# Two weight sums of a Strassen-Winograd pair traced together and pinned in VectorE's order

## The chip, the cores and the metric

One core of a Trainium2 chip runs one launch of the kernel. The metric is device time in microseconds. The kernel before took 2118.74 us (median of three runs, 2118.1 to 2118.84).

## What is computed

One encoder layer on 1024 tokens of width 2048, all in fp32:

```
mod = silu(c) @ w_ada + b_ada;  shift, scale, gate = split(mod, 3)
h = rmsnorm(x, pre_g) * (1 + scale) + shift
q, k, v, gate_a, u, gate_p = split(h @ w_in)          # 4608 columns
y_a = windowed_gqa(q, k, v, rel_table, sink) * silu(gate_a)   # 8 heads, window 128
y_p = multiscale_pool(u, w_pool_grp, pool_scale) * silu(gate_p)
g_a, g_p = split(sigmoid(h @ w_merge + b_merge))      # 2 x 2048 columns
merged = g_a * (y_a @ w_br_attn) + g_p * (y_p @ w_br_pool)
out = x + gate * rmsnorm(merged @ w_out, post_g)
```

## The kernel before

Every big product is done in fp32 precision by splitting each operand into two float32r parts, `hi` and `lo`, and adding three products (hi·hi, hi·lo, lo·hi). A split (`split`, lines 95 to 100) is one ScalarE copy that makes `hi` and one VectorE subtraction that makes `lo`. On top of that each block of 256 output columns, called a *pair*, is one step of Strassen-Winograd multiplication on 2 x 2 blocks: seven block products where plain multiplication has eight. The generator `strassen` (lines 213 to 298) makes a pair. The moving operands (the seven combinations of the activations, `B11`, `T3`, `T2`, `B21`, `T4`, `T1`, `B22`) are prepared once and stay; the weights are loaded for every pair as four blocks A11, A21, A12, A22 in two tiles called `raw`, and the sums of them that the products need are made on VectorE:

- the first product, B11, takes A11 itself;
- the second, T3, takes S3 = A11 - A21, made at line 265 into a tile called `ws`;
- the third, T2, takes A21 + A22 - A11, made by an addition into A21 (line 267) and a subtraction into A11 (line 268);
- the others take A12, A22, the sum in A21, and A12 less the sum in A11.

`prep` splits such a block, giving tiles `whi` and `wlo` (four buffers each, so weights are split some three products ahead of TensorE). `product` runs its matmuls: with four tiles of 128 rows (nj = 4) twelve matmuls of 512 columns, first eight with `whi`, then four with `wlo`. `first_weights` (lines 260 to 269) is a generator that yields the weights of the first three products in turn; the work for S3 is traced when T3's weights are asked for.

Pairs come in stages. Ten half-depth pairs (nj = 2) open the program; then 29 pairs with nj = 4 do the first half of the depth of the combined projection (pass 1), 34 do the second half and add the first (pass 2), and 16 do the two branch projections. 79 pairs thus have nj = 4. `run` (line 325) steps a pair through seven places. At place 2 it finishes the product B22 of the pair before, so that TensorE sees B11, T3, B22 of the pair before, T2, B21, T4, T1. At chosen places it also runs a step of side work: in pass 1 weighted column sums of the modulation weights (`weigh`, line 500), in pass 2 the attention, unit by unit (`step`, line 1087), and then the pooling. In the attention stretch side steps stand at places 0, 1, 3, 4 and 6. A step of attention transposes the probabilities of the unit before (PT, line 1060), forms its scores (SCORE, lines 1037 to 1039, two PSUM banks), takes their maximum on VectorE (line 1043), the exponential on ScalarE (line 1046), a sum with the sink's share (lines 1047, 1048), a reciprocal on VectorE (line 1049) and a scaling on ScalarE (line 1050); every other step also multiplies by the values (PV, lines 1070 to 1072).

The order of each engine's instructions is set by the scheduler of the tile layer, which may move an instruction ahead of others if nothing that it depends on forbids it. `keep` (line 91) forbids it for one instruction: it is placed behind the instruction that was traced just before it on its engine. The weighings of pass 1 are all kept so, and with them what is kept behind them.

Of the kernel before, what the change touches and what calls it, by code (L numbers as in the profile page):

```python
# [43 lines left out]
def encoder_layer(ctx: ExitStack, tc: tile.TileContext, x, c, table, w_ada, b_ada, pre_g,  # L44
# [32 lines left out]
    def uid(s):  # L77
        cnt[0] += 1
        return f"{s}_{cnt[0]}"

    def bank(tag, name="b"):
        return psum.tile([P, 512], F32, tag=tag, name=uid(name), bufs=1 if tag in SEEDED else 2)
# [8 lines left out]
    def keep(ins):  # L91

        tc.keep_in_program_order(ins)

    def split(hi, lo, src, pin=False):
        ins = (nc.scalar.activation(hi, src, AF.Copy),  # L96
               nc.vector.tensor_tensor(lo, src, f32(hi), ALU.subtract))  # L97
        if pin:
            keep(ins[0])
            keep(ins[1])  # L100

    def add(o, a, b, eng=None):
        return (eng or nc.vector).tensor_tensor(o, a, b, ALU.add)  # L103

    def sub(o, a, b):
        return nc.vector.tensor_tensor(o, a, b, ALU.subtract)
# [74 lines left out]
    def load_raws(w, n0, rows, js, pin=False):  # L181

        raws = []
        nj = len(js)
        joint = wp.tile([P, 2, nj, 256], F32, tag="raw", name=uid("raw"), bufs=4) if nj < 4 else None
        for kh in range(2):
            r = joint[:, kh] if nj < 4 else wp.tile([P, nj, 256], F32, tag="raw", name=uid("raw"), bufs=4)
            ins = load(r, rows(w, js, kh)[:, :, n0:n0 + 256])
            if pin:
                keep(ins)  # L190
            raws.append(r)
        return raws
# [13 lines left out]
    def load_parts(ev, part):  # L206
        parts = {}
        for blk in ("22", "21", "11", "12"):
            parts[blk] = ev.tile([P, 512], F32, tag="ev", name=uid("part"))
            load(parts[blk], part(blk))  # L210
        return parts

    def strassen(w, n0, rows, js, op, ev, finish, part=None, raws=None, given=()):

        nj = len(js)
        raws = raws or load_raws(w, n0, rows, js)
        a11, a21, a12, a22 = (raws[kh][:, :, nt * P:(nt + 1) * P] for kh in range(2) for nt in range(2))
        parts = load_parts(ev, part) if callable(part) else part

        def prep(src):
            hi = wp.tile([P, nj, P], F32R, tag="whi", name=uid("whi"), bufs=4)
            lo = wp.tile([P, nj, P], F32R, tag="wlo", name=uid("wlo"), bufs=4)  # L230
            split(hi, lo, src)
            return hi, lo

        def product(wts, mov, ps, fresh=False):
            hi, lo = wts
            for n, (w_, m_) in enumerate(((hi, 0), (hi, 1), (lo, 0))):
                for i, j in enumerate(js):
                    nc.tensor.matmul(ps, w_[:, i], op[mov][j][m_], start=fresh and i == 0 and n == 0,  # L238
                                     stop=i == nj - 1 and n == 2, skip_group_check=True)

        def new(name):
            return ev.tile([P, 512], F32, tag="ev", name=uid(name))

        def read(name, blk, ps):

            t = new(name)
            if part is None or name == "u2":
                nc.scalar.activation(t, ps, AF.Copy)  # L248
                ps = t
            if part is not None:  # L250
                add(t, ps, parts[blk])
            return t

        def result(blk, ps):
            if part is None:
                finish(blk, ps, None, new("c"))
            else:
                finish(blk, ps, parts[blk], parts[blk])

        def first_weights():  # L260
            yield from given
            if not given:
                yield prep(a11)
                s3 = wp.tile([P, nj, P], F32, tag="ws", name=uid("ws"))
                sub(s3, a11, a21)
                yield prep(s3)
            add(a21, a21, a22)
            sub(a11, a21, a11)
            yield prep(a11)

        wts = first_weights()
        pairs_[0] += 1
        bx, bz, bv = bank("mm", "X"), bank(SEEDED[pairs_[0] % 2], "Z"), bank("mm", "V")
        product(next(wts), "B11", bx, True)
        nc.scalar.activation(bz, bx, AF.Copy)
        yield
        product(next(wts), "T3", bv, True)
        p7 = read("p7", "22", bv)
        yield
        product(next(wts), "T2", bz)  # L280
        u2 = read("u2", "21", bz)
        yield
        product(prep(a12), "B21", bx)
        result("11", bx)
        sub(a12, a12, a11)
        yield
        product(prep(a22), "T4", bv)
        finish("21", bv, u2, u2)
        yield
        product(prep(a21), "T1", bz)  # L290
        u4 = new("u4")
        nc.scalar.activation(u4, bz, AF.Copy)
        add(p7, p7, u4)
        finish("22", None, None, p7)
        yield
        product(prep(a12), "B22", bz)
        result("12", bz)
        yield
# [177 lines left out]
    def modulation(j, tile_of, pin=False):  # L476

        st_ = {}

        def step(q, between=None):  # L480
            if q == 0:
                st_["pv"] = bank("at", "GEMV")
            pv = st_["pv"]
            for kc in range(4 * q, 4 * q + 4):
                g = kc % 4 * 32
                ins = nc.tensor.matmul(pv[g:g + 32, :], scz[:, kc, :], tile_of(kc), start=kc < 4,
                                       stop=kc >= 12, tile_position=(0, g))
                if pin:
                    tc.keep_in_program_order(ins)
            if q == 3:  # L490
                acc = xa2.tile([P, 4, P], F32, tag="acc", name=uid("acc"), bufs=2)
                tc.keep_in_program_order(
                    nc.scalar.activation(acc, pv.rearrange("p (g n) -> p g n", g=4), AF.Copy))
                if between:
                    between()
                mod_columns(j, sum_columns(acc))

        return [partial(step, q) for q in range(4)]
# [178 lines left out]
    s0, s1, s2, s3 = modulation(0, ada[0].__getitem__, True)  # L677
# [19 lines left out]
    s0, s1, s2, s3 = modulation(1, ada[1].__getitem__, True)  # L697
# [541 lines left out]
    for b, w in enumerate((w_ba, w_bp)):  # L1239
# [56 lines left out]
        for i in range(8):  # L1296
            def finish(blk, ps, addend, res, gates=gates, shut=shut, open_gate=open_gate, i=i, b=b):
                gt = gates.pop((i, blk))
                if ps is not None and addend is None:
                    keep(nc.vector.tensor_tensor(res, ps, gt, ALU.mult))  # L1300
                else:
                    if ps is not None:
                        add(res, ps, addend)
                    keep(nc.vector.tensor_tensor(res, res, gt, ALU.mult))
                if b == 0:
                    store(block(mp_d, i * 256)(blk), res)
                else:
                    dst = sums_to.pop((i, blk))
                    add(dst, dst, res)
                    if blk[1] == "2":  # L1310
                        store(block(m_d, i * 256)(blk), dst)
                    if to_sum:
                        fetch_sum(*to_sum.popleft())
                if shut:
                    open_gate()
                if wanted:
                    fetch_gate(*wanted.popleft())
# [321 lines left out]
```

## Time and profile before

| what | value |
|---|---|
| median of three runs | 2118.74 us |
| the profiled execution, its own time | 2117.89 us |
| its span, first to last instruction | 2116.1 us |
| TensorE busy, share of the span | 98% |
| VectorE busy | 73% |
| ScalarE busy | 52% |

Read it so: the span and the execution's own time differ by 1.8 us, which lie outside the instructions. In lines of the profile PE is TensorE's matmuls, PEld its weight loads, DVE VectorE, ACT ScalarE, POOL GpSimd, SP the queue of most DMAs. L106, L103, L97 and L96 are helper lines (subtraction, addition, the two halves of a split), so the names of the tiles tell which work it is. A grouped row ends in "busy us, mean ns of one | idle us before it and who ended it". Tile names are cut of their numbers there: `p<-p,u` is the addition of u4 to p7 after T1.

### The profile page before, as it was taken

How to read it: one execution, taken by the hardware profiler on the slowest of the kernel's cores; microseconds unless marked ns; L12 is line 12 of the kernel's file. 1: busy time of each engine (PE TensorE's matmuls, PEld its weight loads, DVE VectorE, ACT ScalarE, POOL GpSimd, SP SyncE). 2: the span in 40 equal slices, each digit the busy share in tenths (PEclk: the TensorE clock that was granted, in tenths of full speed). 3: DMA queues.
4: the chain of work that ended last, by engine and by line, in shares of the span. 5: the costliest groups of instructions: out<-in, count | busy, mean ns of one | idle time of the engine just before them, and what ended most of it. 6: DMA issues, size and time to landing. Idle time of an engine off the chain costs nothing.

```text
span 2116.1 us, 29011 instructions
## 1 busy us (share of the span) xinstructions
PE 2083.9 (98%) x9573; PEld 1715.0 (81%) x9573; DVE 1541.3 (73%) x2771; ACT 1106.8 (52%) x2106; POOL 20.1 (1%) x90
## 2 busy tenths in 40 slices
PE   6999999999999999999999999999999999999998
PEld 4688888888888888888888888888788788888887
DVE  5787667777546776677777677866957977879667
ACT  4654444443366544666655543333645644767554
POOL 0000000000000000000000000000000000000000
PEclk9999999999999999999999999999999999999999
DMA  9886666899767456544645476776755566686897
GB/s 330 278 268 226 205 192 208 292 306 324 255 194 238 149 177 203 171 158 158 197 149 163 156 230 216 219 233 197 237 173 160 184 193 194 220 316 217 294 321 249
DMA packets 302998, 468.20 MB, mean 221 GB/s; under 512 B 24138, under 2 KB 145122, under 8 KB 302848
## 3 DMA queue, kind: packets, MB, share of 16 engines
q1 hardware_dynamic: 299472, 457.82, 66.5%
q0 software_dynamic: 3040, 8.48, 1.0%
q8 instruction: 75, 1.23, 0.2%
q14 instruction: 75, 0.61, 0.1%
q10 hardware_dynamic: 336, 0.06, 0.0%
HBM read 341.45 MB, written 126.90 MB: 221 GB/s over the span
## 4 chain that ended last, share of the span: by engine, by line
PE 91%; DMA 5%; DVE 2%; ACT 1%; issue 1%; SPq 0%; DVEq 0%; POOL 0%; ACTq 0%; POOLq 0%
PE Z L238 31%; PE X L238 20%; PE V L238 20%; PE Z L1349 2%; PE Z L1351 2%; PE Z L1350 2%; DMA ada<-in_w_ada_dram 2%; DMA xt<-in_x_dram 1%; PE V L1351 1%; PE X L1351 1%; PE V L1349 1%; PE X L1349 1%; PE X L1350 1%; PE V L1350 1%; PE PT L1060 1%
## 5 line engine op out<-in xcount | busy, mean ns | idle before, releaser
L96 ACT ACTIVATE whi<-raw 128x512 fp32r<-128x512 f32 (+1 forms) x532 | 322.0, 606 | 508.8 <-PE Z L238 252.0
L97 DVE TENSOR_TENSOR wlo<-raw,whi 128x512 fp32r<-128x512 f32 (+1 forms) x532 | 347.8, 658 | 164.5 <-PE Z L238 122.7
L97 DVE TENSOR_TENSOR wlo<-wr,whi 128x512 fp32r<-128x512 f32 x224 | 150.6, 690 | 51.2 <-ACT whi L96 44.9
L96 ACT ACTIVATE whi<-wr 128x512 fp32r<-128x512 f32 x224 | 138.3, 629 | 86.0 <-DVE wlo L97 31.9
L103 DVE TENSOR_TENSOR raw<-raw,raw 128x512 f32<-128x512 f32 x79 | 54.6, 691 | 106.2 <-DMA raw<-in_w_merge_dram 82.0
L238 PE MATMUL V<-T3h,whi 128*128 128x512 f32 x334 | 91.4, 392 | 1.7 <-DVE u L103 1.2
L238 PE MATMUL Z<-T1h,whi 128*128 128x512 f32 x334 | 91.5, 392 | 0.9 <-ACT u L248 0.9
L238 PE MATMUL Z<-T2h,whi 128*128 128x512 f32 x334 | 91.2, 392 | 0.3 <-ACT whi L96 0.3
L238 PE MATMUL X<-B11h,whi 128*128 128x512 f32 x334 | 91.3, 391 | 0.0
L96 ACT ACTIVATE whi<-ws 128x512 fp32r<-128x512 f32 (+1 forms) x88 | 53.5, 608 | 72.0 <-PE X L238 63.9
L238 PE MATMUL Z<-B22h,whi 128*128 128x512 f32 x334 | 91.1, 392 | 0.0
L238 PE MATMUL V<-T4l,whi 128*128 128x512 f32 x334 | 90.7, 390 | 0.3 <-DVE T4l L97 0.2
L238 PE MATMUL X<-B21h,whi 128*128 128x512 f32 x334 | 90.8, 391 | 0.0
L238 PE MATMUL Z<-T2h,wlo 128*128 128x512 f32 x334 | 90.3, 390 | 0.5 <-DVE wlo L97 0.5
L238 PE MATMUL V<-T3l,whi 128*128 128x512 f32 x334 | 90.5, 390 | 0.2 <-DVE T3l L97 0.2
L238 PE MATMUL V<-T4h,whi 128*128 128x512 f32 x334 | 90.6, 391 | 0.0
L238 PE MATMUL Z<-T1l,whi 128*128 128x512 f32 x334 | 90.4, 390 | 0.1
L238 PE MATMUL X<-B11l,whi 128*128 128x512 f32 x334 | 90.4, 390 | 0.0
L238 PE MATMUL Z<-T1h,wlo 128*128 128x512 f32 x334 | 90.3, 390 | 0.0
L238 PE MATMUL X<-B11h,wlo 128*128 128x512 f32 x334 | 90.2, 390 | 0.0
L238 PE MATMUL Z<-B22l,whi 128*128 128x512 f32 x334 | 90.2, 390 | 0.0
L238 PE MATMUL X<-B21l,whi 128*128 128x512 f32 x334 | 90.2, 389 | 0.0
(358 smaller groups left out, 4840.4 us busy)
## 6 DMA issues: line engine op xcount, KB each, us to landing
part<-part_d SPq DMA_DIRECT2D x136, 256.0 KB, 5.1
ada<-in_w_ada_dram SPq DMA_DIRECT2D x128, 256.0 KB, 5.4
raw<-in_w_merge_dram SPq DMA_DIRECT2D x64, 512.0 KB, 5.8
raw<-in_w_in_dram SPq DMA_DIRECT2D x62, 512.0 KB, 4.2
wr<-ws_dS SPq DMA_DIRECT2D x60, 512.0 KB, 5.5
wr<-in_w_out_dram SPq DMA_DIRECT2D x48, 512.0 KB, 5.3
proj_d<-part SPq DMA_DIRECT2D x68, 256.0 KB, 2.2
sw<-in_w_out_dram SPq DMA_DIRECT2D x64, 256.0 KB, 6.1
```

The lines of the kernel that those rows point to most:

```text
L96: ins = (nc.scalar.activation(hi, src, AF.Copy), nc.vector.tensor_tensor(lo, src, f32(hi), ALU.subtract))
L97: nc.vector.tensor_tensor(lo, src, f32(hi), ALU.subtract))
L103: return (eng or nc.vector).tensor_tensor(o, a, b, ALU.add)
L238: nc.tensor.matmul(ps, w_[:, i], op[mov][j][m_], start=fresh and i == 0 and n == 0, stop=i == nj - 1 and n == 2, skip_group_check=True)
L1060: nc.tensor.transpose(pt[:, i * P:(i + 1) * P], p[:, i * P:(i + 1) * P], ident)
L1349: nc.tensor.matmul(pb, hi, w[0], start=first, stop=False, skip_group_check=True)
L1350: nc.tensor.matmul(pb, lo, w[0], start=False, stop=False, skip_group_check=True)
L1351: nc.tensor.matmul(pb, hi, w[1], start=False, stop=last, skip_group_check=True)
```

## The change

```diff
             if not given:
                 yield prep(a11)
                 s3 = wp.tile([P, nj, P], F32, tag="ws", name=uid("ws"))
-                sub(s3, a11, a21)
+                ins = sub(s3, a11, a21)
+                if nj == 4:
+                    keep(ins)
+                    keep(add(a21, a21, a22))
                 yield prep(s3)
-            add(a21, a21, a22)
+            if nj < 4:
+                add(a21, a21, a22)
             sub(a11, a21, a11)
             yield prep(a11)
```

In every pair with nj = 4 the subtraction that makes S3 is now kept behind the VectorE instruction traced just before it, and the addition into A21 is traced right behind that subtraction, and kept there, instead of being traced after S3's split. No instruction is added or taken away. Which instruction stands just before depends on `run`: where place 0 has no side step it is the `lo` half of A11's split; where it has one, it is the last VectorE instruction of that side step.

The listings below give each engine's instructions in their order, by source line; in those of after, lines behind the change have numbers higher by 4.

On VectorE, in pass 1, at a pair whose place 0 has a side step (its weights are raw_2068 and raw_2070, in the listing after raw_2069 and raw_2071; `p_509` is p7 of the pair before, `acc` the weighed sum). Before, the two sums stand far ahead, the subtraction first:

```order
L106 TENSOR_TENSOR ws_2185<-raw_2068 128x512
L103 TENSOR_TENSOR u_489_1935<-V_1869,u_489_1935 128x512
...
L103 TENSOR_TENSOR raw_2068<-raw_2068,raw_2070 128x4x128
...
L97 TENSOR_TENSOR wlo_2164<-raw_2068,whi_2163 128x512
L106 TENSOR_TENSOR raw_2068<-raw_2068 128x4x128
L97 TENSOR_TENSOR wlo_2188<-ws_2185,whi_2187 128x512
```

After:

```order
L97 TENSOR_TENSOR wlo_2164<-raw_2069,whi_2163 128x512
L103 TENSOR_TENSOR u_518_2090<-V_2006,u_518_2090 128x512
L509 SCALAR_TENSOR_TENSOR acc_1998<-ada_2001,sc,acc_1998 128x512 x2
L509 SCALAR_TENSOR_TENSOR acc_1998<-ada_2047,sc,acc_1998 128x512 x2
L103 TENSOR_TENSOR p_509_2043<-p_509_2043,u_528_2156 128x512
L106 TENSOR_TENSOR ws_2185<-raw_2069 128x512
L103 TENSOR_TENSOR raw_2069<-raw_2069,raw_2071 128x4x128
L97 TENSOR_TENSOR wlo_2189<-ws_2185,whi_2188 128x512
```

The subtraction has moved from ahead of the pair's A11 split to behind four weighings and behind the addition of u4, which needs the pair before to have finished T1.

On VectorE, in the attention stretch, at its second pair (weights raw_8514 and raw_8516; ISA rows are the maximum over scores and the read of its result). Before, the subtraction stands beside the attention step of a whole pair earlier:

```order
L103 TENSOR_TENSOR m_8156<-m_8156 128x1
L106 TENSOR_TENSOR ws_8568<-raw_8514 128x512
L1049 RECIPROCAL m_8156<-m_8156 128x1
...
L103 TENSOR_TENSOR raw_8514<-raw_8514,raw_8516 128x4x128
...
L97 TENSOR_TENSOR wlo_8530<-raw_8514,whi_8529 128x512
```

After, it stands behind the reciprocal of the step of its own place 0 (SCORE_8556, m_8561):

```order
L1047 ISA p_8560,m_8561<-SCORE_8556,bt_8006,nsink_t 128x384
L1047 ISA m_8561 128x1
L97 TENSOR_TENSOR pp_8491<-PT_8546,pp_8490 128x3x128
L1047 ISA p_8615,m_8616<-SCORE_8611,bt_8002,nsink_t 128x384
L1047 ISA m_8616 128x1
L103 TENSOR_TENSOR m_8561<-m_8561 128x1
L1053 RECIPROCAL m_8561<-m_8561 128x1
L106 TENSOR_TENSOR ws_8568<-raw_8514 128x512
L1086 TENSOR_TENSOR g_8225<-PV_8589,g_8225 128x128
L103 TENSOR_TENSOR raw_8514<-raw_8514,raw_8516 128x4x128
L1086 TENSOR_TENSOR g_8227<-PV_8589,g_8227 128x128
L97 TENSOR_TENSOR wlo_8572<-ws_8568,whi_8571 128x512
```

On TensorE, at the same pair, between the end of B11 and the first matmul of T3. Before, one transpose and one set of scores stand there:

```order
L238 MATMUL X_8526<-B11h_6822,wlo_8530 128x512
L1060 MATMUL PT_8546<-ident,p_8428 128x128 x3
L1037 MATMUL SCORE_8556<-k_8030,qhi_8552 128x384
L1038 MATMUL SCORE_8556<-k_8031,qhi_8552 128x384
L1039 MATMUL SCORE_8556<-k_8030,qlo_8553 128x384
L238 MATMUL V_8528<-T3h_6827,whi_8570 128x512
```

After, the attention work that stood behind T3, B22 and T2 has been drawn ahead of T3 by the scheduler: three more sets of scores, the nine PV matmuls and one more transpose:

```order
L1043 MATMUL SCORE_8556<-k_8031,qlo_8553 128x384
L1041 MATMUL SCORE_8611<-k_8031,qhi_8498 128x384
...
L1041 MATMUL SCORE_8667<-k_8031,qhi_8552 128x384
...
L1075 MATMUL PV_8589<-pp_8491,v_8142 128x256
L1076 MATMUL PV_8589<-pp_8490,v_8143 128x256
...
L1064 MATMUL PT_8605<-ident,p_8506 128x128 x3
L1041 MATMUL SCORE_8720<-k_8031,qhi_8498 128x384
...
L238 MATMUL V_8528<-T3h_6827,whi_8571 128x512
```

Over the whole program the subtraction stands, before, ahead of the u4 addition of the pair before it in all 79 pairs. After, it stands behind that addition in 21: six pairs of pass 1 (every other one of its first thirteen pairs), the first pair of pass 2, the 13 attention pairs, and the first pair of the first branch projection. In one of the 13 attention pairs (the sixth) the last VectorE instruction of place 0 is a gate multiplication that waits for little, and T3 follows its scores at once as before. In the first pair of the branch projection the subtraction stands behind the preparation of B21 and T4 of the new activations, and so behind the part addition that reads B22 of the pair before. In the other 58 pairs both sums stand right behind A11's split, one to three products ahead of T3.

## The prediction

> **What bounds the kernel now.** I read the page first: busy shares and the chain that ended last.
>
> ```profile
> PE 2083.9 (98%) x9573; PEld 1715.0 (81%) x9573; DVE 1541.3 (73%) x2771; ACT 1106.8 (52%) x2106; POOL 20.1 (1%) x90
> ...
> PE 91%; DMA 5%; DVE 2%; ACT 1%; issue 1%; SPq 0%; DVEq 0%; POOL 0%; ACTq 0%; POOLq 0%
> ```
>
> TensorE is busy for 98% and is 91% of the chain. VectorE, on which the change acts, is 2% of it. Then the table by stage, for the opening, for all pairs with nj = 4, and for the attention stretch (columns: length, then busy us of PE, PEld, DVE, ACT, POOL; then granted clock, DMA share, GB/s).
>
> ```profile
> 0.00:130.00 130.00, 109.06 (x558) 75.96 (x559) 89.73 (x216) 77.24 (x169) 3.61 (x46) 0.97 0.91 298
> 165.00:1800.00 1635.00, 1631.47 (x7506) 1355.82 (x7505) 1173.76 (x2091) 811.50 (x1522) 3.41 (x19) 1.00 0.64 205
> 880.00:1215.00 335.00, 334.13 (x1740) 286.67 (x1739) 245.73 (x624) 201.04 (x469) 0.14 (x2) 1.00 0.51 164
> ```
>
> From 165 to 1800 us TensorE is idle for 1635.00 - 1631.47 = 3.53 us in all. That bounds any gain: nothing the change does to VectorE can save more than 3.5 us, 0.17%. And TensorE has no slack there: each time a product waits for its weights the whole wait is added to the end. So the question is only whether T3, the product that S3 feeds, now waits.
>
> VectorE does wait for the weights' loads at these sums (who waited, for whom: us in total, times, longest):
>
> ```profile
> DVE raw L103 <- DMA raw<-in_w_merge_dram: 82.0, 27, 8.3
> ...
> DVE ws L106 <- DMA raw<-in_w_merge_dram: 25.4, 10, 5.0
> ```
>
> The sums stand so early in its order that loads have often not landed. Later sums will wait less, but these waits end long before TensorE needs anything, as the 3.53 us say; shortening them earns nothing.
>
> **The change, part by part.** No instruction is added, and no DMA is issued by the moved steps; two sums of some 0.69 us move within VectorE's order. In 58 of the 79 pairs they now stand right behind A11's split, a product or more ahead of T3. I cost these at nothing: a product takes 2.72 us (below), the two sums 1.3. The loads of later weights move by some places in SP's queue, since buffers come free a little differently; they were issued a pair ahead, and I cost that at nothing too, 0 to 1 us. If that cover were gone, the DMA waits above would pass to TensorE.
>
> *Attention, 12 pairs.* TensorE at the second attention pair, where T3 follows PT and SCORE at once:
>
> ```profile
> 919.39 0.49 PE L1060 MATMUL PT<-ident,p 128*128 128x128 f32 x3
> 919.64 0.42 PE L1037 MATMUL SCORE<-k,qhi 128*128 128x384 f32 x1
> ...
> 920.07 0.34 PE L1039 MATMUL SCORE<-k,qlo 128*128 128x384 f32 x1
> 920.25 1.08 PE L238 MATMUL V<-T3h,whi 128*128 128x512 f32 x4
> ...
> 922.98 0.28 PE L1070 MATMUL PV<-pp,v 128*128 128x256 f32 x1
> ...
> 924.06 0.49 PE L1060 MATMUL PT<-ident,p 128*128 128x128 f32 x3
> 924.31 0.42 PE L1037 MATMUL SCORE<-k,qhi 128*128 128x384 f32 x1
> ```
>
> The scores end at 920.07 + 0.34 = 920.41 and T3 starts at 920.25. After the change S3 cannot be made before these very scores have passed through maximum, exponential, sum and reciprocal. The same steps, one unit on, on VectorE and ScalarE:
>
> ```profile
> 921.46 0.61 DVE L1043 CUSTOM_DVE_ANT_0 p<-SCORE,bt,nsink_t 128x384 f32<-128x384 f32 x1
> ...
> 922.00 0.09 DVE L1043 DVE_READ_ACCUMULATOR2_ANT m<- 128x1 f32 x1
> ...
> 922.12 0.62 ACT L1046 ACTIVATE p<-p,m 128x384 f32<-128x384 f32 x1 [1.28 <-DVE m L1043]
> 922.64 0.19 ACT L1046 ACTIVATION_READ_ACCUMULATOR p<-p,m 128x1 f32 x1
> 922.73 0.28 ACT L1047 ACTIVATE m<-sink_t,m 128x1 f32<-128x1 f32 x1
> ...
> 923.04 0.16 DVE L103 TENSOR_TENSOR m<-m 128x1 f32<-128x1 f32 x1 [0.96 <-ACT m L1047]
> ...
> 923.24 0.17 DVE L1049 RECIPROCAL m<-m 128x1 f32<-128x1 f32 x1
> ```
>
> and the means of the rest over this stretch (pp is the probabilities' split, q the queries'):
>
> ```profile
> L97 DVE TENSOR_TENSOR pp<-PT,pp 128x384 fp32r<-128x384 f32 x48 | 26.5, 553 | 1.3 <-ACT pp L96 1.2
> L1050 ACT ACTIVATE p<-p,m 128x384 f32<-128x384 f32 x48 | 29.6, 617 | 7.5 <-DVE m L1049 7.5
> L1016 DVE SCALAR_TENSOR_TENSOR qlo<-qr,qhi 128x512 fp32r<-128x512 f32 x14 | 9.6, 688 | 0.0
> L106 DVE TENSOR_TENSOR ws<-raw 128x512 f32<-128x512 f32 x13 | 8.9, 687 | 0.0
> L1015 ACT ACTIVATE qhi<-qr 128x512 fp32r<-128x512 f32 x14 | 8.7, 624 | 0.0
> L96 ACT ACTIVATE whi<-ws 128x512 fp32r<-128x512 f32 x13 | 8.0, 618 | 0.1
> ```
>
> VectorE's new order there is maximum and read (921.46 to 922.09: 0.63), pp 0.55, the next maximum and read 0.63, addition and reciprocal (923.04 to 923.41: 0.37), S3 0.69: with a hop of 0.1 from TensorE, S3 is ready 2.97 us after the scores. ScalarE must by then have done the second exponential (begun when the second read ends, at 1.91; with its read 0.71) and the scaling (0.62): free at 3.25, then `whi` 0.62, and a hop of 0.1: T3 can start at 3.97 after the scores, 4.1 after its place before. (The hops are an estimate; 922.09 to 922.12 and 923.01 to 923.04 are 0.03.)
>
> TensorE fills part of this with the attention work drawn ahead: three score sets (919.64 to 920.25: 0.61 each), the PV set (922.98 to 924.06: 1.08), one PT (924.06 to 924.31: 0.25): 3.16 us. **T3 waits 4.1 - 3.16 = 0.95.** That order holds in 4 of the 12 pairs: 3.8 us. Three pairs have a third maximum and read ahead of the reciprocal (+0.63) and four score sets with two PTs as cover (2.44 + 1.08 + 0.50 = 4.02): 0.7, together 2.1. Three have a query split in the way, +0.69 on VectorE and up to two copies of 0.62 on ScalarE, behind the same 3.16 of cover or, with narrow scores at a sequence's end, less: 1.6, 1.6 and 2.4, together 5.6. One has a split of the values (+0.69) against some 3.4 of cover: 1.4. The last, which has no scores left to draw on, has the pp splits, S3 and `whi` (0.5 + 0.55 + 0.69 + 0.62 and hops) against one PT and a third of a PV set: 1.8. Sum for attention: **14.7 us**. From below it is 0, if the cover holds; from above 12 x 4.1 = 49, if none does. I take the sum, since each duration in it has a row.
>
> After T3 nothing is late: A11's second split follows within 3 us, and T2 is two products off.
>
> *Pass 1, six pairs.* The rows of one such place, and means of 300 to 480 us:
>
> ```profile
> 434.62 1.07 PE L238 MATMUL X<-B11h,whi 128*128 128x512 f32 x4
> ...
> 434.82 0.60 ACT L292 ACTIVATE u<-Z 128x512 f32<-128x512 f32 x1
> ...
> 437.34 1.07 PE L238 MATMUL V<-T3h,whi 128*128 128x512 f32 x4
> ```
>
> ```profile
> L505 DVE SCALAR_TENSOR_TENSOR acc<-ada,sc,acc 128x512 f32<-128x512 f32 x21 | 15.7, 748 | 0.1
> L103 DVE TENSOR_TENSOR p<-p,u 128x512 f32<-128x512 f32 x10 | 6.9, 689 | 0.0
> ```
>
> B11 starts when T1 ends and lasts 437.34 - 434.62 = 2.72. Behind it: u4's copy (0.20 + 0.60), the addition (0.69), S3 (0.69), `whi` (0.62), three hops: 3.1, so T3 waits 0.4. The four weighings ahead (4 x 0.75 = 3.0) start with T4's end, 2.72 before T1's, and can hold the addition by 0.1 to 0.2 more, a late load of theirs by more. I take 0.45 x 6 = **2.7** (0 to 9, a product's length of 1.5 at most each).
>
> *The first pair of the branch projection.*
>
> ```profile
> 1495.37 1.07 PE L238 MATMUL Z<-B22h,wlo 128*128 128x512 f32 x4
> ...
> 1498.09 1.07 PE L238 MATMUL V<-T3h,whi 128*128 128x512 f32 x4
> ```
>
> S3 now stands behind the addition that reads this B22. It ends at 1496.44; the addition, two subtractions and S3 take four times 0.69 less some overlap, to 1499.1, `whi` to 1499.8: 1.7 after T3's place. I take **1.7** (0 to 3). At the first pair of pass 2 the subtraction stands behind no such addition; 0.
>
> Sum: 14.7 + 2.7 + 1.7 = 19.1 us on the profiled execution's 2117.89, 2137.0; the median of the runs is 0.85 above that execution, so 2137.8, say **2137**.
>
> **The rivals.** *The cover holds (not slower).* If hops are nothing and a scaling goes ahead of the second exponential, or the drawn-ahead pieces run slower than in their old places, T3 finds S3 ready in attention. It decides at 4.1 us of work per pair between scores and T3: 3.16 to 4.02 stand there. For it: TensorE waits nowhere in this stretch now, behind the same chains. Then only pass 1 and the branch pair remain, 2118.74 + 4.4 at most, about 2121.
>
> *The cover fails.* The pieces drawn ahead need VectorE too: a third score set needs a bank that a maximum has emptied, PV needs the pp splits, PT the scaling. Where TensorE, which takes them in order, waits for each, nothing is covered: 49 + 4.4 gives 2172; half of it 2155. Against it: by the rows above the second maximum is done before the third score set is due.
>
> *The clock falls with the waits.* In the opening, with 21 us idle, the granted clock was 0.97 over 130 us, 3.9 us lost, 0.19 us for each idle us; 19 us of waits would cost 3.6 more: 2141. [...]
>
> *Faster, or the pin does nothing.* VectorE's 82 us of waits for loads shrink, but only 3.53 us of TensorE's idle time can come back: 2115.2 at best, within 0.2%.
>
> **How the numbers follow.** My measurement can tell 0.2% (4.2 us) from no change. Forecast, T3 waiting in attention, 2126 to 2150: 0.70. Cover holds, 2121: 0.12. Cover fails by half or more, 2155 to 2172: 0.11. Clock, 2141 or more: 0.04. Faster: 0.03. So slower 0.85, same 0.12, faster 0.03. The range, 2122 to 2157, leaves out part of the covered and half of the uncovered case.
>
> **What would show it.** TensorE's waits in 880 to 1240 us should grow from under 1 us to about 15, on the V matmuls that take T3 with `whi`, put down to ScalarE's split of `ws`, in 12 places of 0.5 to 2.5 us; pass 1 should show six waits of some 0.5 us. The stretches 1215 to 1450 and the last one should keep their lengths. The granted clock should stay 1.00. I am wrong if the waits fall on SCORE, PV or PT instead (cover fails), if VectorE's waits for loads turn up as TensorE's, or if T2 waits.

## The result and the profile after

The changed kernel takes **2139.14 us** (median of five runs, 2137.14 to 2139.89) where the kernel before takes 2118.74 (median of five, 2118.1 to 2121.35): 1.0092 times as long, 95% interval 1.0080 to 1.0104. The forecast was 2137. The profiled execution took 2139.84 us, with a span of 2138.0, 21.9 more than before.

The page of the changed kernel: busy shares, the engines of the chain that ended last, and two of the costliest groups.

```profile
PE 2095.1 (98%) x9573; PEld 1716.6 (80%) x9573; DVE 1545.3 (72%) x2771; ACT 1095.7 (51%) x2106; POOL 20.2 (1%) x90
...
PE 89%; DVE 3%; ACT 2%; DMA 1%; issue 1%; DVEq 0%; SPq 0%; ACTq 0%
...
L96 ACT ACTIVATE whi<-ws 128x512 fp32r<-128x512 f32 (+1 forms) x88 | 53.5, 608 | 100.4 <-DVE ws L106 63.2
L238 PE MATMUL V<-T3h,whi 128*128 128x512 f32 x334 | 93.7, 399 | 9.5 <-ACT whi L96 7.6
```

The last of these rows before the change:

```profile
L238 PE MATMUL V<-T3h,whi 128*128 128x512 f32 x334 | 91.4, 392 | 1.7 <-DVE u L103 1.2
```

The instructions are the same and the shares nearly so; TensorE is still 89% of the chain. What is new is in the last row: T3 waits 7.6 us for the split of `ws`, and that split in turn waits for `ws` itself (63.2 us, most of it harmless). The pairs with nj = 4 (length, busy us of PE, PEld, DVE, ACT, POOL, then granted clock, DMA share, GB/s):

```profile
165.00:1800.00 1635.00, 1620.66 (x7411) 1339.23 (x7410) 1161.51 (x2066) 789.00 (x1503) 3.42 (x19) 1.00 0.63 202
```

From 165 to 1800 us TensorE's idle time has gone from 3.53 to 14.34 us. That is 10.8 us; the span grew by 21.9. So half of the loss does not show as idle time. To find it I set the start of T1 in every pair against its start in the trace before; the difference is the lag up to that pair. This is worked out from the records of the two traces, with no line of a view that prints it:

| stretch | lag gained, us | forecast |
|---|---|---|
| opening, up to the first pairs (nothing changed there; -0.4 to 2.1 in the other kernels) | 0.62 | 0 |
| pass 1, all but its end | 6.46 | 2.7 |
| end of pass 1 (one pair's wait for ScalarE, -0.6 to 2.3 us in the other kernels) | 0.62 | 0 |
| attention | 13.16 | 14.7 |
| pairs behind attention | -0.87 | 0 |
| branch projections | 1.95 | 1.7 |
| sum | 21.94 | 19.1 |

In between the lag stays flat to 0.01 us for up to twelve pairs at a time: what the change costs falls in single pairs.

**Attention.** One window from T1 of the last pair without attention to T1 of the last one with it, before and after:

```profile
886.38:1219.27 332.89, 332.02 (x1727) 284.84 (x1725) 242.38 (x612) 196.43 (x457) 0.14 (x2) 1.00 0.51 165
```

```profile
894.08:1240.12 346.04, 340.68 (x1726) 284.93 (x1725) 241.06 (x615) 193.05 (x459) 0.14 (x2) 1.00 0.49 158
```

The window is 13.15 us longer: 4.49 us more idle (0.87 to 5.36) and 8.66 us more "busy" for as many matmuls (1727 and 1726) at the same clock of 1.00. A matmul's row ends some 0.16 us after the next one has started (PV below: starts 0.12 apart, 0.28 long), so a pause of up to that length leaves no idle time in the row. Counted from start to start in both windows, against the usual spacing of each kind of matmul, the pauses ahead of V matmuls grow by 5.5 us, ahead of PT by 2.8, of PV by 2.7 and of SCORE by 2.7; the rest changes by -0.6. Together these are the 13.15. The waits that do show, who waited for whom, in us, times, longest:

```profile
PE V L238 <- ACT whi L96: 2.2, 6, 0.7
PE PT L1064 <- ACT p L1054: 1.0, 3, 0.4
PE PV L1074 <- ACT pp L96: 0.5, 1, 0.5
PE PT L1064 <- ACT pp L96: 0.5, 1, 0.5
PE PV L1075 <- DVE m L103: 0.4, 1, 0.4
PE SCORE L1041 <- DVE m L1047: 0.2, 1, 0.2
```

Less than half of this is on T3; the rest is on the pieces that were drawn ahead of it. Yet T3 itself starts 0.05 us behind the end of its `whi` in ten of the 12 pairs, also where its row shows no wait. The eleventh attention pair is such a one: `whi` ends at 1173.53 + 0.64 = 1174.17, and T3 follows at 1174.22.

```profile
1173.53 0.64 ACT L96 ACTIVATE whi<-ws 128x512 fp32r<-128x512 f32 x1
...
1173.67 0.55 PE L1064 MATMUL PT<-ident,p 128*128 128x128 f32 x3 [0.34 <-ACT p L1054]
...
1174.22 0.97 PE L238 MATMUL V<-T3h,whi 128*128 128x512 f32 x3
```

The second attention pair, the one that the prediction worked through:

```profile
928.76 0.34 PE L1043 MATMUL SCORE<-k,qlo 128*128 128x384 f32 x1
...
929.13 0.62 DVE L1047 CUSTOM_DVE_ANT_0 p<-SCORE,bt,nsink_t 128x384 f32<-128x384 f32 x1 [1.62 <-PE SCORE L1043]
...
930.57 0.28 PE L1076 MATMUL PV<-pp,v 128*128 128x256 f32 x1
930.69 0.28 PE L1074 MATMUL PV<-pp,v 128*128 128x256 f32 x1
...
930.91 0.16 DVE L1053 RECIPROCAL m<-m 128x1 f32<-128x1 f32 x1
931.00 0.68 DVE L106 TENSOR_TENSOR ws<-raw 128x512 f32<-128x512 f32 x1
...
931.92 0.61 ACT L96 ACTIVATE whi<-ws 128x512 fp32r<-128x512 f32 x1
...
932.59 1.20 PE L238 MATMUL V<-T3h,whi 128*128 128x512 f32 x4 [0.16 <-ACT whi L96]
```

The chain is there link by link: the scores end at 929.10, S3 starts right behind the reciprocal, `whi` behind S3 (0.24 us later, since ScalarE has the scaling to finish), T3 behind `whi`, 3.49 us after the scores (forecast 3.97).

**Pass 1.** The first pair with the new place. u4's copy ends at 203.09, but the last two weighings hold VectorE until the addition of u4 can start at 203.46; S3 and `whi` follow, and T3 starts at 205.52 where B11 would have let it start at 202.29 + 2.72 = 205.01:

```profile
202.00 1.54 DVE L509 SCALAR_TENSOR_TENSOR acc<-ada,sc,acc 128x512 f32<-128x512 f32 x2
202.29 1.07 PE L238 MATMUL X<-B11h,whi 128*128 128x512 f32 x4
202.49 0.60 ACT L296 ACTIVATE u<-Z 128x512 f32<-128x512 f32 x1 [4.84 <-PE Z L238]
...
203.46 0.68 DVE L103 TENSOR_TENSOR p<-p,u 128x512 f32<-128x512 f32 x1
204.06 0.68 DVE L106 TENSOR_TENSOR ws<-raw 128x512 f32<-128x512 f32 x1
...
204.84 0.63 ACT L96 ACTIVATE whi<-ws 128x512 fp32r<-128x512 f32 x1 [1.75 <-DVE ws L106]
```

Four such pairs gain 0.64 to 0.65 us each, a fifth 0.45. The sixth gains **4.22**:

```profile
401.84 0.68 DVE L103 TENSOR_TENSOR p<-p,u 128x512 f32<-128x512 f32 x1
402.44 1.28 DVE L509 SCALAR_TENSOR_TENSOR gacc<-gada,sc,gacc 128x1024 f32<-128x1024 f32 x1
...
403.63 0.68 DVE L106 TENSOR_TENSOR ws<-raw 128x512 f32<-128x512 f32 x1
...
405.03 1.67 PE L238 MATMUL V<-T3h,whi 128*128 128x512 f32 x4 [2.31 <-ACT whi L96]
...
409.48 0.85 PE L238 MATMUL Z<-B22h,whi 128*128 128x512 f32 x3
```

There the place is behind weighings of 1,024 columns, one of them (1.28 us) even behind the addition of u4. T3 waits 2.31 us and then takes 409.48 - 405.03 = 4.45 us instead of 2.72. Three windows around it say why (the third number from the end is the granted clock; the windows are cut where the clock changes in this trace, at 405.53 and 408.94, 3.41 us apart):

```profile
402.12:405.53 3.41, 1.11 (x5) 0.64 (x4) 3.38 (x5) 1.73 (x3) 0.00 (x0) 1.00 1.03 394
405.53:408.94 3.41, 3.41 (x10) 2.63 (x9) 2.57 (x4) 0.00 (x0) 0.00 (x0) 0.50 0.94 282
408.94:412.36 3.41, 3.41 (x16) 2.79 (x16) 1.52 (x3) 2.67 (x5) 0.00 (x0) 1.00 1.03 368
```

The clock fell to half behind the wait, for one such window: 1.73 us on top of it.

**The first pair of the branch projection** waits twice: T3 for `ws`, as forecast, and B21 for A12's split, which stands on ScalarE behind the copies that prepare T1's activations:

```profile
1519.97 1.20 PE L238 MATMUL V<-T3h,whi 128*128 128x512 f32 x4 [1.72 <-ACT whi L96]
...
1526.29 0.62 ACT L96 ACTIVATE T1h<-y 128x512 fp32r<-128x512 f32 x1
1526.81 0.62 ACT L96 ACTIVATE whi<-raw 128x512 fp32r<-128x512 f32 x1
...
1527.48 1.19 PE L238 MATMUL X<-B21h,whi 128*128 128x512 f32 x4 [1.72 <-ACT whi L96]
```

### The profile page after: what moved, and what is told of

Read it like the earlier page. It is cut to its first block, busy times and chain, and to the rows that moved or that the text cites. A ratio compares the mean times of both kernels' runs of the same rounds, so it can differ in the third digit from the quotient of the medians.

```text
span 2138.0 us, 28944 instructions
## 1 busy us (share of the span) xinstructions
PE 2095.1 (98%) x9573; PEld 1716.6 (80%) x9573; DVE 1545.3 (72%) x2771; ACT 1095.7 (51%) x2106; POOL 20.2 (1%) x90
## 4 chain that ended last, share of the span: by engine, by line
PE 89%; DVE 3%; ACT 2%; DMA 1%; issue 1%; DVEq 0%; SPq 0%; ACTq 0%
PE Z L238 30%; PE V L238 21%; PE X L238 20%; PE Z L1353 2%; PE Z L1354 2%; PE Z L1355 2%; PE V L1354 1%; PE V L1355 1%; PE X L1354 1%; PE X L1355 1%; PE X L1353 1%; PE V L1353 1%; PE PT L1064 1%; ACT whi L96 1%; DVE acc L509 0%
## 5 line engine op out<-in xcount | busy, mean ns | idle before, releaser
L96 ACT ACTIVATE whi<-raw 128x512 fp32r<-128x512 f32 (+1 forms) x532 | 316.4, 605 | 413.5 <-PE Z L238 205.7
L103 DVE TENSOR_TENSOR u<-V,u 128x512 f32<-128x512 f32 x94 | 64.7, 688 | 92.6 <-PE V L238 92.2
L296 ACT ACTIVATE u<-Z 128x512 f32<-128x512 f32 x88 | 52.5, 597 | 125.3 <-PE Z L238 121.2
L96 ACT ACTIVATE whi<-ws 128x512 fp32r<-128x512 f32 (+1 forms) x88 | 53.5, 608 | 100.4 <-DVE ws L106 63.2
L238 PE MATMUL V<-T3h,wlo 128*128 128x512 f32 x334 | 90.6, 391 | 0.0
L238 PE MATMUL Z<-T2l,whi 128*128 128x512 f32 x334 | 90.2, 389 | 0.0
```

The costliest lines, as they stand in the source:

```text
L96: ins = (nc.scalar.activation(hi, src, AF.Copy), nc.vector.tensor_tensor(lo, src, f32(hi), ALU.subtract))
```

## The experiments

My theory: where the pin puts S3 behind the side step of place 0, T3 waits for the chain of that step, pair by pair, and nothing else costs. Rivals: the trace order of the two sums; a pin as such; the loads; the clock. Times are medians; ratios are to the kernel before on the same chip.

**Which part of the change costs: trace order, pin or place.** The first kernel takes both pins away and keeps the trace order:

```diff
-                ins = sub(s3, a11, a21)
+                sub(s3, a11, a21)
                 if nj == 4:
-                    keep(ins)
-                    keep(add(a21, a21, a22))
+                    add(a21, a21, a22)
```

> The addition into A21 is traced right behind S3 as in the change, but neither is kept. Mine (the pin costs, the trace order nothing): the scheduler takes the sums ahead again and the time is that of the kernel before, 2118.7 (2117 to 2120.5), with TensorE's waits on whi from ws under 1 us. Rival, the order of the two sums costs (A21 earlier than VectorE needs it): 2125 to 2139.

Measured: 2117.66 us (ten runs, 2113.47 to 2118.84), ratio 0.9993 (0.9983 to 1.0002). Between 165 and 1800 us TensorE waited 1.3 us, and nowhere for `whi`. The trace order costs nothing.

The second keeps both pins and traces the sums before the weights of B11 are given out, so ahead of the side step of place 0:

```diff
-                yield prep(a11)
+                first = prep(a11)
                 s3 = wp.tile([P, nj, P], F32, tag="ws", name=uid("ws"))
                 ins = sub(s3, a11, a21)
                 if nj == 4:
                     keep(ins)
                     keep(add(a21, a21, a22))
+                yield first
                 yield prep(s3)
```

> Both sums are kept, in the same order, but traced right behind A11's split and ahead of the side step of place 0. Mine (the place behind the side step costs, not that the sums are kept): 2119 (2117.5 to 2121). Rival, a kept sum costs wherever it stands, because the scheduler can no longer place it around waits for loads: 2128 to 2139, with VectorE waiting for raw at these sums and TensorE for whi in many pairs.

Measured: 2116.77 us (ten runs, 2114.76 to 2117.76), ratio 0.9992 (0.9983 to 1.0001). In the attention stretch TensorE is never idle:

```profile
880.00:1215.00 335.00, 335.00 (x1748) 288.06 (x1747) 245.37 (x624) 202.34 (x470) 0.14 (x2) 1.00 0.51 165
```

A pin costs nothing in itself that the time shows: one `yield` decides over 20 us. In one place the early sums still came late: in the second pair of the branch projections T3 waited 1.78 us and the pair gained 1.64 us of lag; the pair before it was 0.90 us ahead.

The third keeps S3 alone; the addition into A21 is free and in its old place:

```diff
                 if nj == 4:
                     keep(ins)
-                    keep(add(a21, a21, a22))
                 yield prep(s3)
-            if nj < 4:
-                add(a21, a21, a22)
+            add(a21, a21, a22)
```

> Only the subtraction that makes S3 is kept; the addition into A21 is traced behind S3's split as in the kernel before, and is free. Mine (the place of S3 alone costs): the time of the changed kernel, 2139 (2137.5 to 2140.5). Rival, the kept addition holds up S3's lo half and T2's weights: 12 to 20 times 0.69 us come back, 2125 to 2131.

Measured: 2139.16 us (2138.17 to 2139.53), ratio 1.0096 (1.0081 to 1.0111). The addition has no share in the loss that the time shows; in this trace attention lost 12.0 us instead of 13.2, so its share there is some 1 us at most.

**Where it costs.** Three kernels leave the change out in some pairs, all by one condition:

```diff
+            pin = nj == 4 and not 46 <= pairs_[0] - 1 <= 58
...
-                if nj == 4:
+                if pin:
                     keep(ins)
                     keep(add(a21, a21, a22))
                 yield prep(s3)
-            if nj < 4:
+            if not pin:
                 add(a21, a21, a22)
```

> The sums are neither kept nor traced together in the 13 attention pairs; everywhere else they stay as in the changed kernel. Mine (S3 behind the attention step of its place 0 makes T3 wait, pair by pair, and nothing else costs): the 13.2 us that the attention stretch lost come back and the rest stays, about 2126 us (2125 to 2127.5), with T1 of the pairs of pass 1 and of the branch projections as late against the kernel before as in the changed one (7.7 us at the end of pass 1). Rival, the loads: if the lag in attention came from loads that the later sums of the earlier pairs shifted, it stays, 2137 to 2140.

Measured: 2125.23 us (2125.06 to 2127.95), ratio 1.0038 (1.0023 to 1.0053). T1 lags 6.4 us at the last pair ahead of attention and gains no more in it (5.9 at its last pair): 13 us came back, and only there.

The same with `pairs_[0] - 1 >= 38` (pass 1 left out):

> The sums are neither kept nor traced together in pass 1; from pass 2 on they stay as in the changed kernel. Mine: the 7.1 us that pass 1 lost come back, 2132 us (2131 to 2133), and attention loses its 13 us as before. Rival, the side steps of pass 1 (the moved weighings and column sums, not T3's waits, cost): some 2 us come back at most, 2137.

Measured: 2132.7 us (2130.76 to 2133.72), ratio 1.0068 (1.0051 to 1.0084). Pass 1 gains no lag, attention gains 12.9 us. By these medians attention costs 2139.1 - 2125.2 = 13.9 and pass 1 2139.1 - 2132.7 = 6.4. Runs of one kernel lie up to 5 us apart, so the lags in the traces are the finer measure of the parts.

The same with `pairs_[0] - 1 != 72` (the first branch pair left out):

> As the changed kernel, but in the first pair of the first branch projection the sums are free. Mine (S3 behind the preparation of the new activations holds T3): the 3.2 us that this pair lost come back there, and the small shifts of the pairs behind it may go too, 2136.3 (2135.5 to 2137.3). Rival, the pair is late for another reason (the activations' own preparation came later): less than 1 us comes back, 2138.5.

Measured: 2138.49 us (2137.23 to 2138.96), ratio 1.0093 (1.0076 to 1.0110). The expectation failed: the pair's own 3.2 us are gone (it is 0.73 us ahead), but the next pair gains 1.93. There S3 is made in time and ScalarE is late:

```profile
1532.68 0.68 DVE L106 TENSOR_TENSOR ws<-raw 128x512 f32<-128x512 f32 x1
...
1534.86 0.61 ACT L96 ACTIVATE B22h<-y 128x512 fp32r<-128x512 f32 x1
...
1535.38 0.58 ACT L280 ACTIVATE Z<-X 128x512 f32<-128x512 f32 x1
...
1535.90 0.61 ACT L96 ACTIVATE whi<-ws 128x512 fp32r<-128x512 f32 x1
...
1536.56 1.20 PE L238 MATMUL V<-T3h,whi 128*128 128x512 f32 x4 [2.06 <-ACT whi L96]
```

`ws` is ready at 1533.36, its split starts at 1535.90, behind ScalarE's preparation of the new activations. The wait of the first pair had covered that. So I freed both pairs (`pairs_[0] - 1 not in (72, 73)`):

> As the changed kernel, but free in the first two pairs of the first branch projection, where freeing the first alone moved the loss to the second. Mine (in the second pair S3 is kept behind the last of the activations' preparation, which the first pair's wait had covered): both losses go, T1 of these pairs is 0.7 us earlier against the kernel before than it was ahead of them, and the time is 2136.0 (2135.0 to 2137.0). Rival, the preparation itself is late there and holds the second pair wherever S3 stands: 2138 to 2139.

Measured: 2137.93 us (2137.39 to 2139.72), ratio 1.0094 (1.0077 to 1.0111). Mine fell here: the two pairs still gain 1.40 us together (2.74 in the changed kernel, 1.20 with the first alone freed), now with T4 of the first waiting 0.6 us and its T1 1.4 us for their activations. The preparation of the activations is itself late at this place; S3's place adds to that 2.74 - 1.40 = 1.3 to 2.74 - 1.20 = 1.5. The times of these two kernels can't be told from that of the changed one.

**The clock.** First the pair with the fallen clock alone is freed (`pairs_[0] - 1 != 21`):

> As the changed kernel, but in one pair of pass 1, the one in which T3 waited 2.31 us and the granted clock then read 0.66, the sums are free. If the wait made the clock fall: 4.2 us come back, 2134.9 (2134.3 to 2135.5), and no window of the trace near that pair shows a clock below 0.97. If the clock fell there for another reason (what else ran, or the time since the start): only the wait of 2.3 to 2.5 us comes back, 2136.7, and the windows still show the fall.

Measured: 2134.44, 2134.95 and 2137.92 us, ratio 1.0081 (1.0064 to 1.0098); a fourth run of 4273 us, twice as long as any other, is left out. That is 1.0081 against 1.0092 with intervals that overlap, so the times alone do not tell 4.2 us from 2.3. The trace does: in that pair all 4.22 us are gone, and the windows from 395 to 420 read a clock of 1.00. At the end of pass 1 this execution lost 1.7 us more than the changed kernel's (the wait for ScalarE of the table above).

Then waits of chosen length, put into the kernel before (`DOSE` gives ten pairs of the branch projections the lengths of their chains, `pb[0]` is the bank of B11):

```diff
-                sub(s3, a11, a21)
+                dose = DOSE.get(pairs_[0] - 1)
+                if dose is not None:
+                    keep(nc.vector.tensor_copy(s3[:, 0], pb[0][:, 0:P]))
+                    for m in dose:
+                        keep(add(s3[:, 0:m], a11[:, 0:m], a21[:, 0:m]))
+                    keep(sub(s3, a11, a21))
+                else:
+                    sub(s3, a11, a21)
```

> The kernel before with ten waits added: in ten pairs of the branch projections S3 is made only after a small copy out of B11's finished bank and a chain of additions of 0, 1, 2, 3, 4, 5, 6, 8, 10 and 14 blocks of 128x128, so that T3 should wait about 1.7, 1.9, 2.05, 2.2, 2.4, 2.6, 2.8, 3.1, 3.5 and 4.2 us (0.2 for the copy, 0.69 for the subtraction, 0.62 for the first half of the split, 0.2 of hops, 0.17 for each block). The question is from which wait on the clock falls. If a wait of 2.3 us does it: the products behind the last six waits take 1.7 us longer each, about 2154 us in all. [...] If waits alone don't do it: 2144, the clock 1.00 behind each.

Measured: 2178.17 us. The waits came out longer than planned, 2.45 to 5.36 us, since the copy out of the bank also had to wait for ScalarE's copy of it (0.6 us). Behind every one of the ten, T3 took at least 4.44 us. The first and one more:

```profile
1538.45 1.84 PE L240 MATMUL V<-T3h,whi 128*128 128x512 f32 x4 [2.45 <-ACT whi L96]
...
1562.15 1.68 PE L240 MATMUL V<-T3h,whi 128*128 128x512 f32 x4 [2.77 <-ACT whi L96]
```

For the short end, the chain starts from p7 of the pair before instead of from the bank (`last[0]`, set behind the addition of u4):

> The kernel before with ten smaller waits added: in ten pairs of the branch projections S3 is made only after the addition of u4 to p7 of the pair before and a chain of additions of 3 to 12 blocks of 128x128, so that T3 should wait from about 1.0 to 2.5 us in steps of 0.15. The question is where the fall of the clock begins. From the waits seen so far (1.7 us: clock 1.00; 2.31 us: the clock fell in three traces and not in a fourth; 2.45 us and more: it fell ten times in ten): the waits up to 1.7 us leave T3 at its 2.72 us, those from 2.4 us on lengthen it by 1.7, and the ones between decide where it begins. If the fall goes by the time since the last one and not by the wait's length, T3 is longer behind some of the short waits as well.

Measured: 2161.29 us. Again longer than planned: 1.72, 1.85, 2.18, 2.31, 2.45 and five of 3.51 to 3.91. Behind the fourth the clock fell, behind the fifth, longer one it did not. The difference shows when the windows are cut at the places where this trace's clock changes and at multiples of 3.413 us from there (the third number is TensorE's busy time):

```profile
1598.92:1602.33 3.41, 1.14 (x5) 0.96 (x6) 3.28 (x6) 2.35 (x4) 0.00 (x0) 1.00 0.46 154
1602.33:1605.74 3.41, 3.41 (x10) 2.63 (x9) 2.62 (x5) 1.15 (x2) 0.00 (x0) 0.50 0.53 158
...
1619.40:1622.81 3.41, 2.75 (x13) 1.94 (x11) 2.58 (x5) 1.79 (x3) 0.00 (x0) 1.00 0.48 168
1622.81:1626.22 3.41, 1.63 (x7) 1.38 (x8) 3.31 (x6) 1.76 (x3) 0.00 (x0) 1.00 0.33 104
```

The wait of 2.31 us lies almost whole in one window, which is idle for 2.27 us. The wait of 2.45 us lies across a border: 0.66 us idle in one window, 1.78 in the next. The last section counts this over all traces.

**Whether the pieces drawn ahead were a cover.** The changed kernel with every matmul of the attention kept in its traced place, so that TensorE's order is again that of before:

```diff
-            nc.tensor.matmul(sps, qhi[:, qs], khi[:, ks], start=True, stop=False)
+            keep(nc.tensor.matmul(sps, qhi[:, qs], khi[:, ks], start=True, stop=False))
...
-                nc.tensor.transpose(pt[:, i * P:(i + 1) * P], p[:, i * P:(i + 1) * P], ident)
+                keep(nc.tensor.transpose(pt[:, i * P:(i + 1) * P], p[:, i * P:(i + 1) * P], ident))
```

(and so for the other matmuls of SCORE and PV).

> As the changed kernel, but every matmul of the attention (SCORE, PT, PV) is kept in its traced place on TensorE, so that none of them can be drawn ahead of T3; the order of TensorE is then that of the kernel before, and S3 stays behind the reciprocal of its place 0. Mine (the pieces drawn ahead covered part of the chain from the scores to S3): without them T3 waits the chain, 0.1 + 0.63 + 1.32 + 0.69 + 0.62 + hops, about 3.4 us, in 12 pairs, two of them 4.1: 42 us where the changed kernel lost 13, so 2168; and waits of 3.4 us make the clock fall, 1.7 us each: 2188 (2180 to 2196). If the cover was worth nothing: 2137 to 2145. If the clock stays full behind these waits: 2168.

Measured: 2190.3 us. TensorE's waits for `whi` in 880 to 1310 us, and the second attention pair again:

```profile
PE V L238 <- ACT whi L96: 40.0, 12, 3.8
```

```profile
933.75 0.34 PE L1043 MATMUL SCORE<-k,qlo 128*128 128x384 f32 x1
...
935.99 0.67 DVE L106 TENSOR_TENSOR ws<-raw 128x512 f32<-128x512 f32 x1
...
936.69 0.63 ACT L96 ACTIVATE whi<-ws 128x512 fp32r<-128x512 f32 x1
...
937.37 1.21 PE L238 MATMUL V<-T3h,whi 128*128 128x512 f32 x4 [3.29 <-ACT whi L96]
```

Now the whole chain stands open: 3.29 us here, 40.0 in 12 places, and behind the 11 of them that are 3.05 us or longer T3 is longer by 1.3 to 2.6 us. Attention loses 63 us instead of 13. The cover is shown, and so is its size: 50 us, of which some 20 are the clock.

**A version for use.** As the kernel with the sums ahead of the side step, but free in the branch projections (`pin = nj == 4 and pairs_[0] - 1 < 72`, and `if pin:`):

> As the kernel in which both sums are kept ahead of the side step of place 0, but free in the two branch projections, where keeping them lost 1.6 us in the second pair. Mine: 2115 (2113.5 to 2117), 1.5 to 3 us below the kernel before, because the second pair no longer waits. Rival, these are shifts of the opening that differ from run to run: 2117 to 2118.5, no difference to the kernel before.

Measured: 2117.03 us (eleven runs, 2114.95 to 2119.73), ratio 0.9994 (0.9985 to 1.0003). The rival holds: none of the three kernels without the loss can be told from the kernel before.

## Why the prediction came true, step by step

- **TensorE has no slack, and each wait of T3 is added whole.** True; the lags are never made up, but for work that moved (below).
- **58 early pairs cost nothing.** True: the lag stays at 7.70 to 7.71 over twelve pairs (eleven of them early; the other is the first pair of pass 2, costed at 0) and at 20.04 over eight others, with both sums pinned. The loads cost nothing either: freeing attention left pass 1's loss as it was, and the other way round.
- **Attention, 14.7 forecast, 13.16 measured.** The mechanism is shown (chain, place, cover). The terms were off by more than their sum: the four plain pairs lost 0.40, 1.17, -0.15 and 1.15 (2.6 in all, forecast 3.8), the three with a third maximum 1.35, 1.35 and 1.51 (4.2, forecast 2.1), the three with a query split 1.55, 1.56 and 1.43 (4.5, forecast 5.6), the one with a values split 0.58 (1.4), the last 1.77 (1.8); the harmless sixth pair is 0.51 ahead. In half of the 12 pairs the wait that shows is not T3's: with a values split and two query splits it is PT's or PV's, of 0.41, 0.41 and 0.34 us, with a third maximum once PT's, 0.26, in one plain pair SCORE's, 0.20, in the last PT's and PV's, 0.45 and 0.47. That is the second rival, "TensorE waits for each" drawn-ahead piece, in a small dose. In ten pairs T3 still starts 0.05 us behind `whi`, so there the chain to S3 decides, and the pieces' stops only use up part of its time. In the plain pair with SCORE's wait and in the last pair the pieces decide; that the last one's 1.8 came out, although T3 is not what waits there, is luck. The chain itself was 0.48 us too long in the pair worked through (3.97 for 3.49).
- **"What would show it" was half wrong.** I asked for 12 waits of 0.5 to 2.5 us on T3, together 15. There are six, 2.2 us in all, and 2.6 us on PT, PV and SCORE, which I had named as a sign of being wrong; 8.66 of the 13.15 us hide in rows called busy. Read by idle time alone, the stretch would seem to have lost a third of what it did. Starts of the same product in both traces tell it.
- **Pass 1, 2.7 forecast, 6.46 measured.** Two terms were too small. The plain pairs lose 0.64, not 0.45: T3 starts 0.51 late, as the weighings hold the addition by 0.37 (I took 0.1 to 0.2), and takes 2.85 us instead of 2.72, as it does behind the waits at full clock (2.84 to 2.89 us, once 3.01). I left out these 0.13 us throughout. And one pair is not like the others: I priced six pairs by one pair's rows (four weighings of 0.75), but the sixth has weighings of 1.28 us, one of them between the addition and S3: 2.47 us of wait. The clock's 1.73 come on top. The remaining differences of pass 1 add up to some -0.8. Those of 1.85 in one pair and of -1.21 and -1.10 in two others are the side work's own matmuls, 16 column sums that moved from the two into the one. The small ones (-0.33, -0.47, -0.15 and 0.65) come with no matmul more or less. The 0.65 is a wait of T2 for its `whi`: in that pair the subtraction into A11 stands on VectorE behind a weighing and sums of the side work. I had named a wait of T2 as a sign of being wrong; it came in this one pair.
- **The clock.** The sum of the forecast has no term for it: I took waits of 0.5 to 2.5 us to leave the clock at full, which no run had shown. In the changed kernel's trace it fell to 0.50 for 3.41 us behind a wait of 2.31 us, and T3 took 4.45 us instead of 2.72. That wait is not enough every time: the same pair has the same wait of 2.31 us in the kernel that keeps S3 alone and in the one that frees two branch pairs, and T3 takes 2.85 and 2.86 us there. So the 1.73 us belong to this execution, and their share in the 21.9 is chance. The rival had 0.04, at 0.19 us for each us of waiting, 3.6 in all; what came was one fall in 21 places, 1.73 us.
- **The branch pair, 1.7 forecast, 1.95 measured for the stage.** T3's wait of 1.72 is the one that I worked out; the pair as a whole lost 3.2, as B21 then waits 1.72 too, and 1.25 come back in later pairs (1.39 at one of them also in the kernel that keeps only the trace order). I said that after T3 "nothing is late"; here the next thing on ScalarE was.

So 19.1 stood for 21.9: attention 1.5 too high, pass 1 3.8 too low, the rest near zero. The runs show the sum to be right by its mechanism in each stage; that the stages' errors partly cancel is luck.

## What to carry to other kernels

A pin says "behind what was traced just before", and where steps are interleaved that is whatever the neighbour step ended with: look up, in the new order, which instruction that is in each kind of place, and price every kind by its own rows. A late operand costs the chain to it less the work that can be drawn ahead, and the cover has stops of its own which no idle time shows, so compare starts of the same product in both traces. And count a wait near 2.3 us or longer dearer than its length: here T3 could take 1.3 to 2.6 us longer behind such a wait, and did so behind all 25 of 2.77 us and more.

## What the runs showed of the hardware

- **The clock fell behind waits that I had taken to leave it at full, and not behind all of one length.** Over all traces here: no fall behind any of the waits of T3 from 0.35 to 2.19 us; five falls in seven behind 2.31 us; one in two behind 2.45; 25 in 25 behind 2.77 us and more.
- **The falls go with where the wait lies on a grid.** In every trace all changes of the granted clock are whole multiples of 3.413 us apart (to 0.01 us; in the changed kernel's the falls at 23.24 and 405.53 us are 382.29 apart, 112 times 3.4133), and from one trace to the next the grid lies at another place. Cut at that grid, the waits separate without exception: before each of the 31 falls one step of the grid holds 1.96 us or more of the wait, and in the waits without a fall no step holds more than 1.79. Between the two nothing was measured. These counts are worked out from the records of the traces; the windows above show three of the places.
- **A fall lasted one step or two.** In 22 of the 31 the clock is at half for 3.41 us, and T3 takes 4.03 to 4.46 us instead of 2.72 (the 0.13 below among them); in the nine where the wait itself runs on for 0.6 us or more into the slow step it is 6.83 us, and T3 takes 5.00 to 5.29.
- **T3 took some 0.13 us longer behind a wait at full clock**: 2.84 to 2.89 us (once 3.01), 2.72 in a stream, and this alike behind 0.35, 1.72, 2.18 and 2.45 us. Its second matmul then started some 0.34 us behind the first, where 0.23 is usual.
- **A loss that is freed may reappear**: the first branch pair, freed, no longer lost its 3.2 us, and the next one gained 1.93.
